# A hybrid decoder block on one Trainium2 core: the gate product in 2x2 blocks with seven block products, its weight sums made by DMA during FF2

## The chip, the core and the metric

The kernel runs on one core of a Trainium2 chip. Its engines are TensorE (PE; its weight loads are listed as PEld), VectorE (DVE), ScalarE (ACT), GpSimd (POOL) and SyncE (SP, which here only issues DMAs). Each works through its own queue of instructions in order; semaphores hold an instruction until what it needs is there, and what stands behind it on that engine waits too. The metric is the device time of one execution in microseconds (us). Times in this document are of the chip.

## What is computed

One decoder layer over 1024 tokens of width 1024 in float32. The last two parts matter here (cut from the reference):

```python
h = h + jnp.concatenate([y_a, y_b, y_c], axis=-1) @ w_out[i]
f = jnp.square(jax.nn.relu(rms_norm(h, norm2_g[i]) @ w_ff1[i]))
h = h + f @ w_ff2[i]
gate = jax.nn.sigmoid(rms_norm(h, norm3_g[i]) @ w_ple_gate[i])
h = h + gate * (p[i] @ w_ple_proj[i])
```

`rms_norm` divides a token's row by the root of its mean square and multiplies by a gain g. `w_ff2` is 4096x1024, `w_ple_gate` 1024x1024.

## The kernel before

Everything is kept transposed: a tile is 128 features by 512 tokens, `h_res[n][h]` is feature block n (0 to 7) of token half h (0 or 1). A float32 product is done as three matmuls on halves of the number: each operand is split into a high part (a copy rounded to `float32r`, by ACT, line 134) and a low part (the rest, by DVE, line 135), and high x high, high x low and low x high are added up in a PSUM bank. There are eight banks. Loads go through SP (`fetch`, `w_pair`), with a pool of buffers for each kind: 4 raw tiles, 22 weight parts, 6 for `sum`, 12 for `tmp`, and 56 slots for h, f and their parts.

*FF1 and FF2 in seven products.* Both work on 2x2 blocks (feature halves by token halves) with seven block products instead of eight, from sums of blocks. FF2's weight sums `w_sums` are made in DRAM by accumulating DMAs of POOL during the attention (`block_sums`); the sums of its other operand are made in FF1 by POOL and stored to `f_dram`. FF2 runs over two chunks c of the inner dimension, in each over seven products p in the order `DOWN`, in each over four output blocks j: 56 steps of 24 matmuls. Products that add to the same bank are mates (`MATE`: 1 and 2, 5 and 3, 7 and 4). Results are added to or taken from `h_res` by DVE (lines 973 to 998), and in the last chunk `finish` squares a finished block on ACT and adds the square to `S3[h]` on POOL.

*The gate.* It is a plain product: for each output block n and token half h 8 x 3 matmuls over all feature blocks k, from parts `h3[k][h]` of h times the gain `g3`, which are split when FF2 is over (line 999). The root of the mean square (`root_of`: four matmuls with a matrix of ones, DVE, a power on POOL, a diagonal on DVE; `spread_root`: a matmul, a copy by ACT to `R3[h]`) is applied after the product, in `gated`: DVE multiplies bank and R3, ACT takes the sigmoid, DVE multiplies by the projection of p (fetched from `pp_dram`) and adds h, and the block is stored, by SP for the last two n and by POOL for the others. The last block goes in two pieces of 256 tokens.

The order of instructions on each engine is fixed at build time by a scheduler that works with its own cost model, from the priorities in which the code is written and from buffers that come free; so code written in one place can stand in another on its engine.

Of the kernel before, what the change touches and what calls it, by code (L numbers as in the profile page):

```python
# [7 lines left out]
F32 = mybir.dt.float32  # L8
# [5 lines left out]
P = 128  # L14
# [3 lines left out]
HT = 512  # L18
# [14 lines left out]
def hybrid_block(ctx: ExitStack, tc: tile.TileContext, a: dict):  # L33
# [92 lines left out]
    g3 = load_const("g3", [P, KT])  # L126
    gq = load_const("gq", [P, 1])
# [790 lines left out]

    h_res = [[None, None] for _ in range(KT)]
    u_sum = [None] * 4  # L920
    h3 = [[None, None] for _ in range(KT)]
    S3 = [late_slot("R", "S3") for _ in range(2)]
    R3 = S3
    DOWN = (1, 5, 2, 3, 6, 7, 4)
    CHUNKS = FT // KC
    steps = [(c, p, j) for c in range(CHUNKS) for p in DOWN for j in range(4)]

    def f_pairs():
        for c in range(CHUNKS):
            for p in DOWN:  # L930
# [33 lines left out]

    seen = [False, False]
    for s, (c, p, j) in enumerate(steps):
# [13 lines left out]
        elif p == 6:  # L980
            subtract(nc.vector, u_sum[j], u_sum[j], bank)
            if last:
                add(nc.vector, h_res[j][1], h_res[j][1], u_sum[j])
                finish(j, 1)
                for h in range(2):
                    t = residual(j + 4, h)
                    subtract(nc.vector, t, t, u_sum[j])
        elif p in (2, 3):
            t = residual(j, p - 2)
            add(nc.vector, t, t, bank)  # L990
            if last and p == 2:
                finish(j, 0)
        else:
            h = 0 if p == 4 else 1
            t = residual(j + 4, h)
            subtract(nc.vector, t, t, bank)
            if last and p != 5:
# [8 lines left out]
    def gated(n, h, g_ps, c):  # L1006
        gt = late_slot("tmp", "gt")[:, c]
        nc.vector.tensor_tensor(out=gt, in0=g_ps, in1=R3[h][:, c], op=ALU.mult)
        nc.scalar.activation(gt, gt, AF.Sigmoid)
        nc.vector.tensor_tensor(out=gt, in0=gt, in1=pps[n, h][:, c], op=ALU.mult)  # L1010
        ot = late_slot("tmp", "ot")[:, c]
        nc.vector.tensor_tensor(out=ot, in0=gt, in1=h_res[n][h][:, c], op=ALU.add)
        queue = nc.sync if n >= KT - 2 else nc.gpsimd
        queue.dma_start(a["out"][n * P:(n + 1) * P, half[h]][:, c], ot)

    pps, undone = {}, []
    for n0 in range(0, KT, 2):
        wus = [plain_units(a["w_ple_gate"][n]) for n in (n0, n0 + 1)]
        for n, h in [(n, h) for h in (1, 0) for n in (n0, n0 + 1)]:
            pps[n, h] = fetch(pp_dram[n][:, half[h]], "sum")  # L1020
            last = n == KT - 1 and h == 0

            for c in (slice(0, 256), slice(256, HT)) if last else (slice(0, HT),):
                g_ps = late_bank("g_ps")[:, c]
                product(g_ps, [(wus[n - n0][k], cols(h3[k][h], c)) for k in range(KT)])
                undone.append((n, h, g_ps, c))
                if n == 0:
                    if h == 0:
                        diag = root_of(S3[0], "30")
                    continue  # L1030
                if n == 1:
                    spread_root(diag, R3[h])
                while undone:
                    gated(*undone.pop(0))
# [62 lines left out]
```

## Time and profile before

| | us |
|---|---|
| three runs | 1264.21, 1258.99, 1256.04 |
| their median | 1258.99 |
| the profiled execution | 1262.6 |
| its span, from first to last instruction | 1260.9 |
| FF2, first to last matmul (span's time) | 860 to 1165 |
| gate stage, to the end of the span | 1165 to 1261 |

The profile is of one execution, with its own time; times in its rows count from the start of its span. A row of a group says line, engine and operation, out<-in by the program's names, the number, and lengths; a row of a wait says who waited for whom, for how long in all and how often. "L135" is line 135 of the kernel above. Idle time of an engine costs only where the others wait for it.

### The profile page before, as it was taken

The numbers are of one execution on the slowest core, as the hardware profiler recorded it, in microseconds if no ns is written. First come the engines' busy times: TensorE is split into PE (matmuls) and PEld (weight loads), VectorE is DVE, ScalarE is ACT, GpSimd is POOL, SyncE is SP. The second block draws the span as 40 slices with busy tenths as digits, with TensorE's granted clock in tenths as the row PEclk, the third lists the DMA queues.
The fourth block names the chain that finished last, engine by engine and source line by source line (L and its number), as shares of the span: only waits on it lengthen the run. The fifth ranks groups of instructions, "written<-read, shape, count | busy, mean of one in ns | idle before, by whom it ended". The sixth has DMA issues, their size and how long they took to land.

```text
span 1260.9 us, 17509 instructions
## 1 busy us (share of the span) xinstructions
PE 1215.0 (96%) x5868; PEld 1034.1 (82%) x5868; DVE 880.7 (70%) x1324; ACT 603.8 (48%) x1167; POOL 364.2 (29%) x365
## 2 busy tenths in 40 slices
PE   9999898899999999879999999999999999999998
PEld 7898798898888878658888888888888888888887
DVE  7746886898979654676887777777755565686443
ACT  7725655666656454553334334344544344555211
POOL 2324434455323212233553453431000000122110
PEclk9999998999999999989999999999999999999999
DMA  9603257788542298689999999958956565653231
GB/s 309 211 18 117 84 158 210 167 210 159 119 114 38 67 292 226 175 221 251 269 244 255 252 244 250 252 193 302 354 179 224 183 223 170 203 166 106 76 111 51
DMA packets 118700, 234.89 MB, mean 186 GB/s; under 512 B 13105, under 2 KB 20529, under 8 KB 118353
## 3 DMA queue, kind: packets, MB, share of 16 engines
q1 hardware_dynamic: 94752, 168.08, 40.4%
q0 software_dynamic: 23856, 65.70, 23.3%
q8 instruction: 46, 0.75, 0.3%
q14 instruction: 46, 0.37, 0.1%
HBM read 176.57 MB, written 78.64 MB: 202 GB/s over the span
## 4 chain that ended last, share of the span: by engine, by line
PE 82%; DVE 8%; DMA 5%; issue 2%; ACT 1%; POOL 1%; SPq 0%; DVEq 0%; POOLq 0%; ACTq 0%
PE d_ps L731 24%; PE f_ps L731 24%; PE qkv_ps L161 3%; PE qkv_ps L162 3%; PE qkv_ps L163 3%; PE g_ps L161 2%; PE g_ps L163 2%; PE g_ps L162 2%; DVE rem L413 2%; PE av L456 2%; DMA S<-sq 2%; PE w_tr L438 1%; PE cv_ps L161 1%; DMA h_dram<-h 1%; PE cv_ps L162 1%
## 5 line engine op out<-in xcount | busy, mean ns | idle before, releaser
L135 DVE TENSOR_TENSOR w_lo<-raw,w_hi 128x512 fp32r<-128x512 f32 x268 | 244.9, 916 | 94.4 <-ACT w_hi L134 92.2
L134 ACT CAST w_hi<-raw 128x512 fp32r<-128x512 f32 x268 | 165.2, 619 | 242.6 <-PE d_ps L731 116.7
L731 PE MATMUL f_ps<-hn_hi,w_hi 128*128 128x512 f32 x448 | 176.5, 394 | 5.3 <-ACT v L884 5.3
L731 PE MATMUL f_ps<-hn_lo,w_hi 128*128 128x512 f32 x448 | 175.7, 392 | 0.0
L731 PE MATMUL f_ps<-hn_hi,w_lo 128*128 128x512 f32 x448 | 175.3, 392 | 0.0
L731 PE MATMUL d_ps<-f_hi,w_lo 128*128 128x512 f32 x448 | 174.3, 389 | 0.0
L731 PE MATMUL d_ps<-f_hi,w_hi 128*128 128x512 f32 x448 | 174.3, 389 | 0.0
L731 PE MATMUL d_ps<-f_lo,w_hi 128*128 128x512 f32 x448 | 174.3, 389 | 0.0
L731 PEld LDWEIGHTS f_ps<-hn_hi,w_hi 128*128 128x128 f32 x448 | 85.1, 190 | 23.4 <-ACT v L884 5.7
L719 POOL TENSOR_TENSOR S<-S,sq 128x512 f32<-128x512 f32 x14 | 22.6, 1614 | 273.5 <-ACT sq L788 273.5
L731 PEld LDWEIGHTS f_ps<-hn_lo,w_hi 128*128 128x128 f32 x448 | 85.1, 190 | 17.9 <-issue 0.2
L731 PEld LDWEIGHTS f_ps<-hn_hi,w_lo 128*128 128x128 f32 x448 | 85.0, 190 | 18.0
L731 PEld LDWEIGHTS d_ps<-f_hi,w_hi 128*128 128x128 f32 x448 | 84.1, 188 | 17.6
L731 PEld LDWEIGHTS d_ps<-f_lo,w_hi 128*128 128x128 f32 x448 | 84.1, 188 | 17.4
L731 PEld LDWEIGHTS d_ps<-f_hi,w_lo 128*128 128x128 f32 x448 | 84.1, 188 | 17.3
L413 DVE TENSOR_TENSOR_SCAN rem<-rem 128x128 f32<-128x128 f32 (+3 forms) x64 | 89.0, 1393 | 11.1 <-ACT rem L409 10.6
L161 PE MATMUL qkv_ps<-whi,xn_hi 128*128 128x384 f32 x256 | 92.0, 359 | 2.6 <-DVE V L138 2.6
L163 PE MATMUL qkv_ps<-whi,xn_lo 128*128 128x384 f32 x256 | 89.8, 351 | 0.0
L162 PE MATMUL qkv_ps<-wlo,xn_hi 128*128 128x384 f32 x256 | 89.8, 351 | 0.0
L135 DVE TENSOR_TENSOR f_lo<-raw,f_hi 128x512 fp32r<-128x512 f32 x112 | 77.6, 723 | 4.6 <-ACT f_hi L134 4.0
L134 ACT CAST f_hi<-raw 128x512 fp32r<-128x512 f32 x112 | 67.0, 620 | 17.9 <-DMA raw<-f_dram 13.4
L416 POOL TENSOR_TENSOR wt<-wt,rem 128x127 f32<-128x127 f32 (+4 forms) x40 | 44.3, 1109 | 107.7 <-DVE rem L413 44.9
(219 smaller groups left out, 2665.7 us busy)
## 6 DMA issues: line engine op xcount, KB each, us to landing
raw<-in_w_ff SPq DMA_DIRECT2D x160, 256.0 KB, 4.1
raw<-f_dram SPq DMA_DIRECT2D x112, 256.0 KB, 4.8
raw<-w_sums SPq DMA_DIRECT2D x64, 256.0 KB, 3.7
f_dram<-f SPq DMA_DIRECT2D x48, 256.0 KB, 4.4
f_dram<-t SPq DMA_DIRECT2D x48, 256.0 KB, 3.9
w_sums<-in_w_ff POOLq DMA_DIRECT2D x8, 1024.0 KB, 11.7
w_sums<-w_sums POOLq DMA_DIRECT2D x8, 1024.0 KB, 12.4
raw<-in_w_ff POOLq DMA_DIRECT2D x32, 256.0 KB, 5.4
```

The source lines that it names most:

```text
L134: nc.scalar.copy(hi, src)
L135: low.tensor_tensor(out=lo, in0=src, in1=hi, op=ALU.subtract)
L161: nc.tensor.matmul(ps, lh, rh, start=first and i == 0, stop=False)
L162: nc.tensor.matmul(ps, lh, rl, start=False, stop=False)
L163: nc.tensor.matmul(ps, ll, rh, start=False, stop=last and i == len(terms) - 1)
L413: nc.vector.tensor_tensor_scan(out=back, data0=back, data1=back, initial=1.0, op0=ALU.mult, op1=ALU.bypass)
L416: done = (nc.vector if on_vector else nc.gpsimd).tensor_tensor(out=wt[:, :W - 1], in0=wt[:, :W - 1], in1=rem[:, 1:W], op=ALU.mult)
L438: nc.tensor.transpose(tr[:, n:n + P], wts[i][:, kb * P:(kb + 1) * P], ident)
L456: nc.tensor.matmul(av[:, first * P:], lhs, part[:, o:o + m], start=kb == 0 and part is hi, stop=kb == 2 * g + 1 and part is lo)
L719: return eng.tensor_tensor(out=out, in0=x, in1=y, op=ALU.add)
L731: nc.tensor.matmul(bank, l, r, start=first and k == 0 and i == 0, stop=k == len(b) - 1 and i == 2, skip_group_check=True)
```

## The change

The gate product is also done with seven block products. With A11 to A22 the blocks of the weight matrix, products 1, 2 and 4 take A11, A12 and A22 as the weight operand, and 5, 6, 7 and 3 take S1 = A21 + A22, S2 = S1 + A11, S3 = A11 + A21 and S4 = S2 + A12; the other operand is blocks of h times `g3` or sums of them, some negated (`minus_g3`), so that every sum is an addition. Three things make the operands:

- *Weight sums.* `gate_sums` makes the four sums in DRAM (`g_sums`) with 32 DMAs of 256 KB through POOL, 16 plain copies and 16 accumulating, two at each of 16 steps of FF2's first chunk, each pair behind a two-column copy on POOL that waits for that step's result.
- *Sums of h.* Four kinds of scaled blocks `hg` (ACT, line 996 of the new code) are added up in place by 16 accumulating DMAs from SBUF to SBUF (`sum_h`), four for each j, each of which needs the one before it for that j to have landed. Products 1, 2 and 3 take single blocks, split as before (`h3_pair`); 6, 5, 7 and 4 take the sums, split by `h3_sum`.
- *FF2's second chunk* runs its products in the order 1, 2, 6, 7, 4, 5, 3, so that token half 0 is done earlier; its root is made within FF2.

The gate's products run in the order 1, 2, 3, 6, 5, 7, 4, each over four output blocks j with 12 matmuls; 7 and 4 do the last block in two pieces.

```diff
+    minus_g3 = const.tile([P, KT], F32, name="minus_g3")
+    nc.vector.tensor_scalar_mul(minus_g3, g3, -1.0)
...
+    G_STEPS = [((0, "A21"), (2, "A11")), ((0, "+A22"), (1, "A11")), ((2, "+A21"), (1, "+S1")),
+               ((3, "A12"), (3, "+S2"))]
+    def gate_sums(i, behind):
+        if not 0 <= i < 16:
+            return
+        paced = nc.gpsimd.tensor_copy(pace, behind[:, :2])
+        with tc.issue_after(paced.ins):
+            for to, what in G_STEPS[i % 4]:
...
+                if what[0] == "+":
+                    nc.gpsimd.dma_start(g_sums[to, j], src, accum_op=ALU.add,
+                                        max_dma_last_dim=2048)
+                else:
+                    nc.gpsimd.dma_start(g_sums[to, j], src)
...
-    DOWN = (1, 5, 2, 3, 6, 7, 4)
+    DOWN = [(1, 5, 2, 3, 6, 7, 4), (1, 2, 6, 7, 4, 5, 3)]
...
+    def scale_h(of, n, h, g):
+        t = scaled[of, n % 4] = slot("hg")
+        nc.scalar.activation(t, h_res[n][h], AF.Copy, scale=g[:, n:n + 1])
+    def h3_pair(p, n, h):
+        h3[p][n % 4] = pair("h3")
+        split(h_res[n][h], *h3[p][n % 4], scale=g3[:, n:n + 1])
+    def sum_h(to, of, j):
+        nc.gpsimd.dma_start(scaled[to, j], scaled[of, j], accum_op=ALU.add)
+    def h3_sum(p, of, j):
+        h3[p][j] = two_parts(scaled[of, j], lambda s: slot(f"h3_{s}", F32R))
...
-    for n, h in [(j + 4 * i, h) for i, h in ((0, 0), (0, 1), (1, 1), (1, 0)) for j in range(4)]:
-        h3[n][h] = pair("h3")
-        split(h_res[n][h], *h3[n][h], scale=g3[:, n:n + 1])
-    diag = root_of(S3[1], "31")
+        if p != 1 and c == 0:
+            gate_sums(s - 12, u_sum[j] if p == 6 else t)
+        if last and p == 5:
+            if j == 1:
+                diag = root_of(S3[0], "30")
+            elif j == 3:
+                spread_root(diag, R3[0])
+        elif last and p == 3:
...
+            for n in range(3) if j == 2 else (3,) if j == 3 else ():
+                scale_h("12", n, 1, minus_g3)
+                sum_h("11", "12", n)
...
+    GATE = (1, 2, 3, 6, 5, 7, 4)
+    MATE = {2: 1, 4: 7}
...
+    for p in GATE:
+        for j in range(4):
+            cs = pieces if p in (7, 4) and j == 3 else whole
...
+            for bank, c in zip(banks, cs):
+                run(bank, w, [cols(b, c) for b in h3[p]], p not in MATE, p not in (1, 7))
+                if p == 1:
+                    v_of[j] = late_slot("tmp", "v")
+                    nc.scalar.copy(v_of[j], bank)
+                elif p == 2:
+                    gated(j, 0, bank, late_slot("tmp", "gt"), c)
+                elif p == 6:
+                    subtract(nc.vector, v_of[j], v_of[j], bank)
+                elif p == 5:
+                    e_of[j] = late_slot("tmp", "e")
+                    add(nc.vector, e_of[j], bank, v_of[j])
+                    t = late_slot("tmp", "gt")
+                    add(nc.vector, t, d_bank.pop((3, j))[0], e_of[j])
+                    gated(j, 1, t, t, c)
+                elif p == 7:
+                    t = e_of[j][:, c]
+                    add(nc.vector, t, bank, t)
+                    gated(j + 4, 1, t, t, c, -1.0)
+                elif p == 4:
+                    t = v_of[j][:, c]
+                    add(nc.vector, t, bank, t)
+                    gated(j + 4, 0, t, t, c, -1.0)
+            if p == 1:
+                if j == 1:
+                    diag = root_of(S3[1], "31")
+                elif j == 3:
+                    spread_root(diag, R3[1])
+                h3_pair(2, j + 4, 0)
+                sum_h("12", "22", j)
+            elif p == 2:
+                h3_pair(3, j + 4, 1)
+                sum_h("22", "11", j)
+            elif p == 3:
+                h3_sum(6, "22", j)
+                sum_h("21", "22", j)
+            elif p == 6:
+                h3_sum(5, "11", j)
...
-        "w_ple_gate": blocks(i["w_ple_gate"][0]),
+        "w_ple_gate": quad_blocks(i["w_ple_gate"][0], 4, 4)[:, 0],
```

How the instructions stand now shows best at three places. On POOL before, around the gate's first stores, there are only the second root r and stores of finished blocks (line numbers of the old code):

```order
L1014 DMA out_T<-ot_11664 128x512
L1014 DMA out_T<-ot_11671 128x512
L169 TENSOR_TENSOR r_11708<-ms_11706,mhalf 128x4
L1014 DMA out_T<-ot_11746 128x512
L1014 DMA out_T<-ot_11753 128x512
```

On POOL in the new order, from the addition of FF2's last square on (line 721; `sq_11616` is of the last step) to the last of the sums (line 1003; `hg_11532` is the last j of the sum that product 6 takes; line numbers of the new code, as in the next fences):

```order
L721 TENSOR_TENSOR S_1911_8639<-S_1911_8639,sq_11616 128x512
L1003 DMA hg_11588<-hg_11530 128x512
L1003 DMA hg_11524<-hg_11619 128x512
L1003 DMA hg_11576<-hg_11528 128x512
L1003 DMA hg_11530<-hg_11522 128x512
L171 TENSOR_TENSOR r_11682<-ms_11680,mhalf 128x4
L1003 DMA hg_11619<-hg_11532 128x512
L1003 DMA hg_11578<-hg_11530 128x512
L1003 DMA hg_11532<-hg_11524 128x512
L1003 DMA hg_11580<-hg_11532 128x512
```

The root for token half 1 stands between sums, each of which waits for the landing of another: `hg_11530` is read by the first sum and written by the fourth, `hg_11619` is written by the one after r, and `hg_11532` needs that one and the second.

On DVE before, at the second half's first evictions, rows of the gate stand beside weight parts, one bank read for every three rows:

```order
L1008 TENSOR_TENSOR gt_11742<-g_ps_11676,S_1910_8634 128x512
L1010 TENSOR_TENSOR gt_11742<-gt_11742,raw_11674 128x512
L1012 TENSOR_TENSOR ot_11746<-gt_11742,h_9156 128x512
L1008 TENSOR_TENSOR gt_11749<-g_ps_11714,S_1910_8634 128x512
L1010 TENSOR_TENSOR gt_11749<-gt_11749,raw_11712 128x512
L1012 TENSOR_TENSOR ot_11753<-gt_11749,h_9207 128x512
```

On DVE in the new order, from the diagonal of the root (which waits for r above) to the first block that is gated (line 1074; `h_lo<-hg` is the low part of a sum of h):

```order
L808 TENSOR_TENSOR diag_11684<-ident,r_11682 128x512
L140 SCALAR_TENSOR_TENSOR h_lo_11804<-h_9005,c_g_115,h_hi_11803 128x512
L140 SCALAR_TENSOR_TENSOR h_lo_11835<-h_9057,c_g_115,h_hi_11834 128x512
L137 TENSOR_TENSOR w_lo_11970<-raw_11967,w_hi_11969 128x512
L140 SCALAR_TENSOR_TENSOR h_lo_11866<-h_9109,c_g_115,h_hi_11865 128x512
L137 TENSOR_TENSOR h_lo_11890<-hg_11526,h_hi_11889 128x512
L137 TENSOR_TENSOR w_lo_11994<-raw_11991,w_hi_11993 128x512
L137 TENSOR_TENSOR h_lo_11914<-hg_11528,h_hi_11913 128x512
L137 TENSOR_TENSOR h_lo_11938<-hg_11530,h_hi_11937 128x512
L137 TENSOR_TENSOR h_lo_11962<-hg_11532,h_hi_11961 128x512
L1074 TENSOR_TENSOR gt_11766<-g_ps_11628,S_1910_8638 128x512
```

The low part of `hg_11532`, the sum that lands last, now stands ahead of the first gated block, and the diagonal ahead of three of the four parts for product 3.

The end of DVE's queue in the new order, from the read of the last bank (the second 256-wide piece of product 4's last block) on:

```order
L721 TENSOR_TENSOR v_11736<-g_ps_12292,v_11736 128x256
L1074 TENSOR_TENSOR v_11736<-v_11736,S_1910_8638 128x256
L1076 TENSOR_TENSOR v_11710<-v_11710,raw_12399 128x512
L1074 TENSOR_TENSOR v_11736<-v_11736,S_1910_8638 128x256
L1076 TENSOR_TENSOR v_11736<-v_11736,raw_12419 128x256
L721 TENSOR_TENSOR v_11710<-v_11710,h_10112 128x512
L721 TENSOR_TENSOR v_11736<-v_11736,h_10166 128x256
L1076 TENSOR_TENSOR v_11736<-v_11736,raw_12419 128x256
L721 TENSOR_TENSOR v_11736<-v_11736,h_10166 128x256
```

Behind that read stand eight more rows, of both pieces and of the block before; before the change three stood behind the last read.

More of the change, by code (lines that the diff above doesn't have):

```diff
@@ L963, in finish @@
         seen[h] = True
+    h3 = {p: [None] * 4 for p in range(1, 8)}
+    scaled = {}
+    def scale_h(of, n, h, g):
[8 more added lines that the diff above has]
+        h3[p][j] = two_parts(scaled[of, j], lambda s: slot(f"h3_{s}", F32R))
     seen = [False, False]
@@ L990, in hybrid_block @@
             add(nc.vector, t, t, bank)
[L991 to L992 removed]
+            if last:
+                finish(j, p - 2)
         else:
@@ L996, in hybrid_block @@
             subtract(nc.vector, t, t, bank)
-            if last and p != 5:
+            if last and p != 7:
                 finish(j + 4, h)
-    for n, h in [(j + 4 * i, h) for i, h in ((0, 0), (0, 1), (1, 1), (1, 0)) for j in range(4)]:
-        h3[n][h] = pair("h3")
-        split(h_res[n][h], *h3[n][h], scale=g3[:, n:n + 1])
-    diag = root_of(S3[1], "31")
[L1006 to L1034, printed above, removed]
+        if p != 1 and c == 0:
+            gate_sums(s - 12, u_sum[j] if p == 6 else t)
```

57 lines of the change are left out of this document (53 added, 4 removed).

## The prediction, made before the changed kernel had run

> **What bounds the kernel now.** I read the page's first parts, then a table of stages, then the product's own rows, and last the waits of the engines that feed it. First the page: the span, the busy time of each engine, and the shares of the chain that ended last.
>
> ```profile
> span 1260.9 us, 17509 instructions
> PE 1215.0 (96%) x5868; PEld 1034.1 (82%) x5868; DVE 880.7 (70%) x1324; ACT 603.8 (48%) x1167; POOL 364.2 (29%) x365
> PE 82%; DVE 8%; DMA 5%; issue 2%; ACT 1%; POOL 1%; SPq 0%; DVEq 0%; POOLq 0%; ACTq 0%
> ```
>
> TensorE carries the end. The stage table (from:to, length, then busy us of PE, PEld, DVE, ACT and POOL, the granted clock, the share of the DMA engines, GB/s) shows the same for a stretch of FF1, two of FF2 and the gate stage:
>
> ```profile
> 600.00:700.00 100.00, 100.00 (x443) 82.84 (x442) 81.26 (x84) 35.98 (x62) 49.83 (x46) 1.00 0.95 255
> 925.00:1012.00 87.00, 87.00 (x385) 72.07 (x384) 49.43 (x78) 36.78 (x62) 0.00 (x0) 1.00 0.60 203
> 1012.00:1165.00 153.00, 153.00 (x679) 126.73 (x677) 103.67 (x153) 75.17 (x127) 21.10 (x13) 1.00 0.53 173
> 1165.00:1261.00 96.00, 91.06 (x429) 75.68 (x427) 41.19 (x63) 16.31 (x27) 10.21 (x15) 0.99 0.23 80
> ```
>
> PE is never idle in FF2 and has 91 of the gate stage's 96 us; DVE is busy in 41 of them, the DMA engines in 23%. So fewer matmuls shorten the gate stage as long as DVE, POOL and the sums keep up. The rows of the two products, and two of the 256-wide matmuls at the end:
>
> ```profile
> L731 PE MATMUL d_ps<-f_hi,w_hi x448: 389/389/390, 860.2 to 1164.2; 128*128 128x512 f32 x150
> L731 PE MATMUL d_ps<-f_hi,w_lo x448: 389/389/390, 860.7 to 1164.6; 128*128 128x512 f32 x150
> L163 PE MATMUL g_ps<-h_hi,w_lo x136: 279/389/398, 1166.2 to 1255.8; 128*128 128x512 f32 x120, 128*128 128x256 f32 x16
> 1250.38 0.28 PE L163 MATMUL g_ps<-h_hi,w_lo 128*128 128x256 f32 x1
> 1250.50 0.28 PE L161 MATMUL g_ps<-h_hi,w_hi 128*128 128x256 f32 x1
> ```
>
> FF2's 3 x 448 = 1344 matmuls last from 860.2 to 1164.6 + 0.4 = 1165.0, so a 512-wide one costs 304.8 / 1344 = 0.227 us; a 256-wide one starts 0.12 after the one before. The gate stage is 360 of the first and 48 of the second kind.
>
> **The matmuls that go.** Seven products of four blocks with 12 matmuls are 336 full ones, of which 24 are cut into 48 halves as before. 312 stay whole: 48 x 0.227 = 10.9 us less on PE. The norm's matmuls stay, a pair of groups like these moving into FF2:
>
> ```profile
> 1165.00 0.79 PE ms_ps L798 x8
> 1176.84 0.86 PE R_ps L813 x2
> ```
>
> PE's gate stage goes from 360 x 0.227 + 48 x 0.12 + 2 x 1.65 = 90.8 us (measured 1165.0 to 1256.1, 91.1) to 79.9; of these 1.65 now lie in FF2, so it ends 78.3 us after FF2's last matmul.
>
> **What DVE gets to do.** Its speed, in rows of start, length, line:
>
> ```profile
> 1165.04 0.69 DVE L716 TENSOR_TENSOR h<-h,d_ps 128x512 f32<-128x512 f32 x1 [0.48 <-PE d_ps L731]
> 1165.64 0.68 DVE L135 TENSOR_TENSOR w_lo<-raw,w_hi 128x512 fp32r<-128x512 f32 x1
> 1166.25 0.16 DVE L801 TENSOR_SCALAR ms<-ms_ps 128x4 f32<-128x4 f32 x1
> 1240.86 0.69 DVE L1010 TENSOR_TENSOR gt<-gt,raw 128x512 f32<-128x512 f32 x1 [0.70 <-ACT gt L1009]
> 1241.58 0.69 DVE L1012 TENSOR_TENSOR ot<-gt,h 128x512 f32<-128x512 f32 x1
> L138 DVE SCALAR_TENSOR_TENSOR h_lo<-h,c_g,h_hi x16: 739/744/1784, 1124.4 to 1167.1; 128x512 fp32r<-128x512 f32 x16
> ```
>
> An operation is 0.69 long, but the next starts 0.60 after it if it doesn't need its result (1165.04 to 1165.64), and 0.72 if it does (1240.86 to 1241.58). After FF2's last step the new order has 121 on DVE: 96 full ones, the diagonal among them (96 x 0.60 = 57.6), 8 of the scaled kind (8 x 0.74 = 5.9), 16 halves (16 x 0.43 = 6.9, lengths in the next fence) and one of 0.16, some 12 of them 0.12 longer for their operand: 72.0 us, against 78.3 on PE. DVE has 6 us to spare, no more; had each cost 0.72, DVE would be the bound. ACT's 80 at 0.63 (sq below) are 50 us, so it has room.
>
> **The tail.** Now, behind the last matmul (1256.1):
>
> ```profile
> 1256.10 0.42 DVE L1008 TENSOR_TENSOR gt<-g_ps,S 128x256 f32<-128x256 f32 x1 [1.08 <-PE g_ps L163]
> 1257.00 0.43 DVE L1010 TENSOR_TENSOR gt<-gt,raw 128x256 f32<-128x256 f32 x1 [0.48 <-ACT gt L1009]
> 1257.46 0.42 DVE L1012 TENSOR_TENSOR ot<-gt,h 128x256 f32<-128x256 f32 x1
> ```
>
> It is 1.8 us to the end of DVE, and 3.0 more to the span's end for the store, which stays. In the new order eight DVE rows stand behind the last read of a bank, six halves and two whole ones, since the two pieces and the block before them are interleaved: 0.43 + 6 x 0.43 + 2 x 0.60 = 4.2, and some 0.5 of backlog from product 5 (five rows for a block, 3.1 us, against 2.7 of PE). So +2.9 us.
>
> **The sums of h by DMA.** Sixteen accumulating DMAs of 256 KB, SBUF to SBUF, go through POOL's queue, with the squares' additions and the root r between them, so one late sum holds all behind it. The like in this trace: S<-sq with its landing, raw<-raw, and for contrast a plain store of POOL and a load of SP; then what stands between the sums.
>
> ```profile
> L790 POOL DMA_DIRECT2D S<-sq x14: 843/857/892, 457.7 to 548.1; - x14
> DMA to landing us min/median/max: 3.4/5.2/8.0
> raw<-raw POOLq DMA_DIRECT2D x32, 256.0 KB, 5.2
> out_T<-ot POOLq DMA_DIRECT2D x12, 256.0 KB, 2.4
> raw<-in_w_ple_gate SPq DMA_DIRECT2D x16, 256.0 KB, 2.6
> L719 POOL TENSOR_TENSOR S<-S,sq x14: 1283/1398/3350, 1068.6 to 1167.5; 128x512 f32<-128x512 f32 x14
> L169 POOL TENSOR_TENSOR r<-ms,mhalf 128x4 f32<-128x4 f32 x2 | 2.1, 1035 | 3.8 <-DVE ms L801 3.7
> L788 ACT ACTIVATE sq<-h x28: 614/632/635, 456.7 to 1165.8; 128x512 f32<-128x512 f32 x28
> ```
>
> I followed POOL's rows one by one with a landing time L, an issue of 0.87, an addition of 1.3 and the root of 1.04. The first sum leaves 11.7 us before FF2's end, as soon as its square and the one before are added. Six landings then stand in a row (each reads or overwrites the one before, or is behind such a one in the queue), with 7.2 us of issues, additions and the root between them and 0.7 for the cast: DVE can take the last block of product 6, the row that waits longest, at 6L - 3.8 after FF2's end, and has 102 rows from there (86 x 0.60 + 12 x 0.12 + 16 x 0.43 = 60). DVE's end by this chain is 6L + 56.2; PE's chain gives 78.3 + 0.5 (PE's wait for the root's matmul, behind r in POOL's queue; 0 to 1) + 4.7 = 83.5. They meet at L = 4.5. Ends of L: 3.4 and 5.2 as a median. In the two stages of those rows the DMA engines are near full (0.95 in 600 to 700), in the gate stage 0.23 before and, with the sums, more weights and as many stores, perhaps half; I take L = 4.0, nearer the low end, and PE's chain holds.
>
> [...]
>
> **The weight sums in FF2.** 32 DMAs of 256 KB, DRAM to DRAM, half of them accumulating, and 16 tiny copies on POOL that pace them, in steps 12 to 27 of the first chunk, 925 to 1012, where POOL is idle (0.00 in the table). Their like are the 1 MB sums of FF2's own weights; beside them what SP's queue took in that window, and what ACT waits for in FF2:
>
> ```profile
> w_sums<-in_w_ff POOLq DMA_DIRECT2D x8, 1024.0 KB, 11.7
> w_sums<-in_w_ff POOLq DMA_DIRECT2D x16, 7.0
> q1 hardware_dynamic: 13438, 24.47, 63.3%
> ACT w_hi L134 <- PE d_ps L731: 116.7, 63, 2.1
> ```
>
> By a quarter of these landings they take up to 16 x 1.8 + 16 x 2.9 = 75 us of the window's 87; by bytes (SP moves 24.5 MB in 63% of 87 us, 0.45 MB/us; these are 8 MB) at least 18. What covers them is that ACT waits 116.7 us in FF2 for PE to free weight buffers: operands stand ready ahead of need. FF1 runs at a share of 0.95 with PE at 100%. I take 0, between 0 and the price of the third case.
>
> **The rest.** The second chunk's new order has the same matmuls, DMAs and additions; the 16 SP loads of each product only move with it, and the gate's first weights stay behind the last of them: 0. The 16 scaled copies lie on ACT, idle half of FF2. The new DVE operation at the start is 0.16 long in an engine that waits for loads there: 0. Twelve more gate weight loads on SP (28 against 16) at 2.6 us each run ahead of PE.
>
> Sum: -10.9 + 2.9 + 0.5 = -7.5. The profiled execution took 1262.6 (its span and 1.7 around it), so 1255.1; it lies 3.6 above the median of 1258.99, and against that the time is 1251.5.
>
> **Rivals.** *Slow sums, DVE the bound.* At L = 5.2 DVE ends 87.4 + 1.65 after FF2's old end instead of 92.9 (1257.9 - 1165.0): -3.8, 1255. At 8.0, the longest landing, +13, 1272. For it: two groups with a median of 5.2. Against: emptier engines. It decides from 4.5 on.
>
> *FF2 starved, the other side.* If the sums keep POOL's ring busy for 75 us and SP's gets half of each engine then, SP's 55 us (63% of 87) find 37 + 12 = 49: 6 short, and at a third 25 + 12 = 37: 18 short, because the accumulating packets are the slower ones. What the buffers held ahead don't cover, PE loses: -7.5 + 6 to + 18, 1257 to 1269, slower than before from a loss of 7.5 on. Against it: the 116.7 us of waiting for buffers. [...]
>
> *The whole saving.* If DVE keeps pace to the end the tail is 2.3 (one operation more): -10.9 + 0.5 = -10.4, 1248.6. The interleaved last rows speak against it.
>
> **The numbers.** The sum with its own bounds (1248 to 1255) has 0.60, slow sums 0.20, FF2 starved 0.13, the whole saving 0.07. The range 1246 to 1261 leaves out the far ends of the second and third. A measurement of this kernel tells about 1% from no change (12.6 us). Nearly all cases lie within it: 0.90; faster by more needs the whole saving and a low median, 0.05; slower takes the far ends, 0.05.
>
> **What would show it.** PE's gate rows end 78 to 80 us after FF2's last; FF2 lasts 306 to 307 us, with the norm's matmuls in it; sums land in 3.4 to 4.5; DVE is busy nearly without a gap from 25 us into the gate stage and ends 4 to 5 us behind PE. I am wrong if PE waits for the low parts of h or w in the gate stage, if DVE's end is 8 us or more behind PE, or if FF2 is longer than 308 us.

## The result and the profile after

The changed kernel takes 1251.85 us (median of 8 runs, 1249.81 to 1253.73), the kernel before 1261.21 in its 8 (1256.04 to 1264.21): a ratio of 0.9934 with a 95% interval of 0.9917 to 0.9952, so 6 to 10.5 us less, 8.3 in the middle. The page of the changed kernel, its span and its engines:

```profile
span 1250.1 us, 17694 instructions
PE 1202.6 (96%) x5820; PEld 1024.0 (82%) x5820; DVE 907.5 (73%) x1374; ACT 626.7 (50%) x1212; POOL 407.7 (33%) x432
```

TensorE still carries the span, with 48 matmuls less for the gate. The rows of the two products (number, lengths, first and last start), and the one wait of TensorE in the gate stage (who for whom, us in all, times, longest):

```profile
L733 PE MATMUL d_ps<-f_hi,w_hi x448: 389/389/791, 856.2 to 1162.0; 128*128 128x512 f32 x150
L733 PE MATMUL d_ps<-f_hi,w_lo x448: 388/389/397, 856.6 to 1162.5; 128*128 128x512 f32 x150
L733 PE MATMUL g_ps<-h_hi,w_lo x120: 279/389/796, 1163.1 to 1242.6; 128*128 128x512 f32 x104, 128*128 128x256 f32 x16
```

```profile
PE R_ps L815 <- DVE diag L808: 1.4, 1, 1.4
```

FF2 lasts from 856.2 to 1162.9 (the last start and 0.4), 306.7; the gate product ends at 1242.6 + 0.28 = 1242.9, 80.0 after it. VectorE's last rows:

```profile
1242.45 0.42 DVE L721 TENSOR_TENSOR v<-g_ps,v 128x256 f32<-128x256 f32 x1
1242.79 0.68 DVE L721 TENSOR_TENSOR v<-v,h 128x512 f32<-128x512 f32 x1
1243.38 0.42 DVE L721 TENSOR_TENSOR v<-g_ps,v 128x256 f32<-128x256 f32 x1
...
1246.72 0.42 DVE L721 TENSOR_TENSOR v<-v,h 128x256 f32<-128x256 f32 x1
```

It ends at 1247.1, 4.3 behind TensorE, and the span 2.9 later with the store. By stages, in the two profiled executions:

| us | before | after | difference |
|---|---|---|---|
| FF2 | 304.8 | 306.7 | +1.9 |
| FF2's last matmul to the gate's last | 91.1 | 80.0 | -11.1 |
| from there to VectorE's end (the tail) | 1.8 | 4.3 | +2.5 |
| from there to the end of the span | 3.0 | 2.9 | -0.1 |
| FF2's start to the end of the span | 400.7 | 393.9 | -6.8 |

The spans differ by 10.8; the other 4.0 lie ahead of FF2, where the two kernels have the same order but for one operation of 0.16 us. Over the fourteen executions profiled here FF2 starts anywhere between 853.6 and 862.1, so those 4 us are taken as scatter, and the change is read from FF2's start on. Next the sums of h with their landing, and three rows of VectorE's timeline (start, length, operation, idle time before it and who ended it): the first waits for one of these sums, the other two for TensorE.

```profile
L1003 POOL DMA_DIRECT2D hg<-hg x16: 859/880/1561, 1149.3 to 1187.0; - x16
DMA to landing us min/median/max: 3.3/4.8/6.3
```

```profile
1187.36 0.69 DVE L137 TENSOR_TENSOR h_lo<-hg,h_hi 128x512 fp32r<-128x512 f32 x1 [4.50 <-ACT h_hi L136]
...
1237.32 0.69 DVE L721 TENSOR_TENSOR v<-g_ps,v 128x512 f32<-128x512 f32 x1 [0.15 <-PE g_ps L733]
...
1240.04 0.69 DVE L721 TENSOR_TENSOR v<-g_ps,v 128x512 f32<-128x512 f32 x1 [0.49 <-PE g_ps L733]
```

They land in 4.8 (median), not in 4.0; the low part of the last block for product 6 comes 1187.36 - 1162.9 = 24.5 after FF2. From there VectorE is busy nearly without a gap until it waits 0.15 and 0.49 for TensorE. The chain of the end, in order of time (start, length, what), shows what stands before TensorE's 1.4 us:

```profile
1170.08 4.86 DMA hg<-hg
1174.93 0.28 issue
1175.22 0.86 POOL hg L1003
1176.08 1.07 POOL r L171
1177.15 0.02 issue
1177.17 0.70 DVE diag L808
1177.88 0.04 issue
1177.92 1.13 PE R_ps L815 x2
1179.05 60.98 PE g_ps L733 x280
```

A sum on POOL waits for another sum's landing, the root r stands behind it in the queue, and diag and TensorE wait for r. The window of the weight sums and the gate stage (columns as in the prediction's table of stages):

```profile
925.00:1012.00 87.00, 87.00 (x386) 72.06 (x385) 48.78 (x77) 35.77 (x60) 27.42 (x47) 1.00 0.94 283
...
1163.00:1250.00 87.00, 78.43 (x370) 65.12 (x368) 71.21 (x121) 37.91 (x67) 20.72 (x29) 0.98 0.58 160
```

The weight sums bring the DMA engines to a share of 0.94, and TensorE has no gap. The 0.58 of the gate stage is a mean over a busy beginning and a quieter end; while the sums of h run, around TensorE's wait, the share is higher:

```profile
1170.00:1174.00 4.00, 4.00 (x19) 3.31 (x18) 1.83 (x4) 3.91 (x7) 2.65 (x3) 1.00 0.91 192
1174.00:1177.00 3.00, 2.48 (x11) 1.70 (x10) 0.00 (x0) 1.66 (x4) 1.78 (x3) 1.00 1.12 202
1177.00:1179.00 2.00, 1.08 (x3) 0.60 (x4) 1.83 (x3) 0.24 (x1) 1.03 (x2) 1.00 0.86 153
1179.00:1182.00 3.00, 3.00 (x15) 2.46 (x14) 3.00 (x6) 0.38 (x1) 1.73 (x2) 1.00 0.90 128
```

(The share is worked out from the times of packets and comes out above 1 in places.)

### The profile page after: what moved, and what is told of

Its sections match the earlier page's. It is cut to its first block, busy times and chain, and to the rows that moved or that the text cites. A ratio compares the mean times of both kernels' runs of the same rounds, so it can differ in the third digit from the quotient of the medians.

```text
span 1250.1 us, 17694 instructions
## 1 busy us (share of the span) xinstructions
PE 1202.6 (96%) x5820; PEld 1024.0 (82%) x5820; DVE 907.5 (73%) x1374; ACT 626.7 (50%) x1212; POOL 407.7 (33%) x432
## 5 line engine op out<-in xcount | busy, mean ns | idle before, releaser
L137 DVE TENSOR_TENSOR w_lo<-raw,w_hi 128x512 fp32r<-128x512 f32 x280 | 249.7, 894 | 92.9 <-ACT w_hi L136 92.3
L136 ACT CAST w_hi<-raw 128x512 fp32r<-128x512 f32 x280 | 171.8, 618 | 215.8 <-PE d_ps L733 118.4
L733 PEld LDWEIGHTS d_ps<-f_lo,w_hi 128*128 128x128 f32 x448 | 84.1, 188 | 17.8 <-issue 0.2
L733 PEld LDWEIGHTS d_ps<-f_hi,w_hi 128*128 128x128 f32 x448 | 84.1, 188 | 17.6 <-ACT hg L996 0.2
L733 PEld LDWEIGHTS d_ps<-f_hi,w_lo 128*128 128x128 f32 x448 | 84.1, 188 | 17.4
L171 POOL TENSOR_TENSOR rs<-ss,mhalf 128x4 f32<-128x4 f32 x32 | 44.4, 1389 | 75.9 <-DVE ss L341 72.4
```

The source lines that it names most:

```text
L136: nc.scalar.copy(hi, src)
L137: low.tensor_tensor(out=lo, in0=src, in1=hi, op=ALU.subtract)
L171: nc.gpsimd.tensor_tensor(out=out, in0=in_, in1=mhalf[:, :n], op=ALU.pow)
L733: nc.tensor.matmul(bank, l, r, start=first and k == 0 and i == 0, stop=k == len(b) - 1 and i == 2, skip_group_check=True)
```

## The experiments

The changed kernel and twelve others, each against the kernel before, with the stages of one profiled execution each (us; "VectorE's end" counts from FF2's last matmul, "rest" from there to the end of the span):

| kernel | ratio, 95% interval | FF2 | gate on TensorE | tail | VectorE's end | rest |
|---|---|---|---|---|---|---|
| changed kernel | 0.9934, 0.9917 to 0.9952 | 306.7 | 80.0 | 4.3 | 84.2 | 2.9 |
| no_h_sums | 0.9947, 0.9929 to 0.9966 | 306.7 | 78.4 | 4.2 | 82.6 | 5.3 |
| late_root | 1.0010, 0.9998 to 1.0022 | 306.7 | 88.3 | 4.3 | 92.5 | 2.9 |
| no_w_sums | 0.9928, 0.9903 to 0.9952 | 306.7 | 79.9 | 4.2 | 84.1 | 4.0 |
| w_sums_twice | 0.9956, 0.9937 to 0.9974 | 307.6 | 81.2 | 4.3 | 85.4 | 3.0 |
| root_first | 0.9928, 0.9909 to 0.9947 | 306.7 | 78.4 | 4.3 | 82.7 | 2.9 |
| extra_landing | 0.9943, 0.9921 to 0.9964 | 306.6 | 79.4 | 4.3 | 83.7 | 2.9 |
| tail_whole | 0.9946, 0.9925 to 0.9967 | 306.7 | 79.2 | 4.1 | 83.3 | 3.3 |
| reorder_only | 1.0029, 1.0014 to 1.0044 | 306.7 | 95.4 | 1.9 | 97.2 | 3.0 |
| sums_on_dve | 0.9963, 0.9943 to 0.9982 | 306.7 | 81.8 | 4.3 | 86.1 | 6.2 |
| block_last | 0.9957, 0.9938 to 0.9975 | 306.7 | 80.7 | 2.4 | 83.1 | 6.8 |
| late_sums | 0.9974, 0.9957 to 0.9990 | 306.7 | 84.4 | 4.3 | 88.7 | 2.9 |
| best | 0.9944, 0.9921 to 0.9967 | 306.6 | 79.0 | 2.4 | 81.4 | 6.8 |

The stages scatter too. Five kernels besides the changed one have its order on POOL and TensorE up to the root of token half 1. TensorE's wait at R_ps is 1.44 in the changed kernel and 1.29, 0.53, 0.73 and 0.31 in no_w_sums, extra_landing, tail_whole and late_sums; in w_sums_twice it is not there, but TensorE stops 0.98 at ms_ps, the matmuls before the root. The order is the same and the waits are not, so a difference of a microsecond between two gate stages is not yet an effect of the edit.

**no_h_sums.** `sum_h` does nothing.

```diff
-        nc.gpsimd.dma_start(scaled[to, j], scaled[of, j], accum_op=ALU.add)
+        pass
```

> Leaves out the sixteen accumulating DMAs that add up the blocks of h, so products 6, 5, 7 and 4 work on single scaled blocks. In the changed kernel 84.2 us pass from FF2's last matmul to the end of VectorE. Theory A (TensorE's chain carries; the sums cost only the 1.4 us that TensorE waits at R_ps for the root that stands behind them on POOL): TensorE's gate part 80.0 -> 78.6, VectorE still ends about 4.3 behind it, 84.2 -> 82.8, the time 1.4 shorter. Theory B (the sums bind through VectorE, which waits 4.5 us for one of them): VectorE ends under 3 us behind TensorE and the 84.2 go below 80.5, the time about 4 shorter.

Theory A holds: 78.4, no wait of TensorE, and a tail of 4.2. VectorE now waits for TensorE (its waits in the gate stage):

```profile
DVE v L718 <- PE g_ps L733: 5.9, 4, 1.6
...
DVE e L721 <- PE g_ps L733: 1.4, 1, 1.4
```

So without the sums VectorE has 7.3 us to spare in products 6 and 5, and the tail is the same with that and without: it isn't work left over from the products before. Only the total doesn't follow (0.9947): the rest is 5.3 instead of 2.9 (last section).

**late_root.** The root of token half 1 later in the code.

```diff
-                if j == 1:
-                    diag = root_of(S3[1], "31")
-                elif j == 3:
-                    spread_root(diag, R3[1])
 ...
                 sum_h("22", "11", j)
+                if j == 3:
+                    diag = root_of(S3[1], "31")
 ...
                 sum_h("21", "22", j)
+                if j == 3:
+                    spread_root(diag, R3[1])
```

> The root of token half 1 and its spreading come later in the code, behind the sums of h (same work, same result). Theory A (TensorE's chain carries, and its 1.4 us at R_ps are the root's place in POOL's queue): no wait at R_ps, TensorE's gate part 80.0 -> 78.6, and since the sums also come 1.1 earlier without the root between them, VectorE's end 84.2 -> 82.8. Theory B (VectorE is already the bound, by the sums): TensorE ends 1.4 earlier but VectorE only 1.1 at most, so its distance behind TensorE grows. Rival C (the wait at R_ps is not POOL's queue): R_ps still waits 1 us or more.

All three theories missed what the edit did: ms, which r needs, came late on VectorE, r stood on POOL behind two stores that wait for VectorE, and TensorE met R_ps before it:

```profile
1197.35 0.15 DVE L803 TENSOR_SCALAR ms<-ms_ps 128x4 f32<-128x4 f32 x1
1197.59 5.63 POOL L171 TENSOR_TENSOR r<-ms,mhalf 128x4 f32<-128x4 f32 x1 [1.08 <-DVE ms L803]
1204.00 2.07 PE L815 MATMUL R_ps<-diag,ones 128*128 128x512 f32 x2 [7.15 <-DVE diag L808]
```

The two stores were out by 1196.5; what r waited for last is ms. It then lasted 5.63, where the six of the changed kernel and the six of the kernel before take 1.0 to 1.9; why is not known, and without it the wait of 7.15 would be some 4 shorter. So the run shows that a late root stops TensorE, but not what this place in the queue alone costs. The gate is 88.3 - 78.4 = 9.9 longer for a wait of 7.15, and the whole gain is gone. The other 2.7 are the clock, at half until 1209 (last section).

**no_w_sums and w_sums_twice.** The weight sums left out, and made twice.

```diff
-        if not 0 <= i < 16:
-            return
+        return
         paced = nc.gpsimd.tensor_copy(pace, behind[:, :2])
 ...
-    ... else g_sums[int(of[1]) - 1, j]
+    ... else w_block("w_ple_gate", "A11", j)
```

```diff
-                if what[0] == "+":
-                    nc.gpsimd.dma_start(g_sums[to, j], src, accum_op=ALU.add, max_dma_last_dim=2048)
+                for sums in (g_sums, g_twin):
+                    if what[0] == "+":
+                        nc.gpsimd.dma_start(sums[to, j], src, accum_op=ALU.add, max_dma_last_dim=2048)
```

> Leaves out the weight sums (the 32 DMAs and 16 paced copies in FF2); the products that need them read another block of the weights. Theory A (the weight sums cost FF2 nothing, though the DMA engines are at a share of 0.94 there): FF2 stays 306.7 within 0.3 and the time within 1 us. Theory B (they starve FF2 a little): FF2 shorter by 0.5 us or more.

> Makes every weight sum twice (a second copy that nobody reads): 64 DMAs instead of 32 in the same steps. By the changed kernel's shares in the window (54% for SP's queue, 39% for POOL's) they want 54 + 79 = 133% of 87 us. Theory A (SP's loads get their turn and only the sums fall behind; weight parts stand ready ahead of need): FF2 stays 306.7 to 307.7. Theory B (loads and sums share the engines alike): SP's queue loses, TensorE waits in FF2, which grows by 5 us or more.

Left out: FF2 is 306.7 as with them (theory A), at a share of 0.61 instead of 0.94 in the window. Twice, in the same window of that run (922 to 1009):

```profile
922.00:1009.00 87.00, 87.00 (x385) 72.06 (x384) 39.99 (x63) 27.62 (x49) 39.16 (x68) 1.00 1.03 307
```

The engines are full, TensorE still has no gap there, and the sums fall behind: the last one is issued at 1037 instead of 1016. The loads of SP's queue fall behind too: ACT's wait for TensorE to free weight buffers, the sign that operands stand ready ahead of need, shrinks from 118.4 over FF2 in the changed kernel to 48.0, and it waits 44.3 for loads of `w_ff` instead. So the stock of parts covers the sums, and doubled they have used up more than half of it; FF2 loses 0.9 later (307.6, within theory A), 0.7 of it behind VectorE. Already the single sums make SP's loads slower: from 925 to 1012 those of `w_ff` land in 5.0 (median) in the changed kernel and in 2.9 in the kernel before, those of `f_dram` in 6.8 and 5.0. How the DMA engines divide their time between the two queues was not shown. The gate stage of this run, 81.2, holds the stop of 0.98 at ms_ps and a stretch at half clock behind it (last section).

**root_first.** One sum issued behind r instead of before it.

```diff
+                if j == 2:
+                    with tc.issue_after(root_ops["31"].ins):
+                        sum_h("22", "11", j)
+                else:
+                    sum_h("22", "11", j)
-                sum_h("22", "11", j)
```

> One sum of h (the one that waits on POOL for another's landing just ahead of the root r of token half 1) is issued after r instead of before it; all else is unchanged. In the changed kernel r starts at 12.9 us after FF2's last matmul, TensorE waits 1.4 at R_ps. Theory A (TensorE's chain carries, the wait is r's place in POOL's queue): r starts 2.5 to 3 us earlier, no wait at R_ps, TensorE's gate part 80.0 -> 78.4 to 78.7, VectorE's end 84.2 -> 82.6 to 82.9, the time 1.4 shorter. Theory B (VectorE is bound by the sums at their landing of 4.8): TensorE gains 1.4, VectorE not more than the 1.1 by which the sums behind r move up, and its waits at the end are gone. Rival C (something else holds R_ps): no change.

Theory A holds: no wait, 78.4, 82.7, so 1.5 us shorter by the stages of one execution each; after the scatter above, the gain can be less in others. The runs (0.9928 against 0.9934) can't tell so little.

**extra_landing and late_sums.** The last sum for product 6 done twice, and four times.

```diff
                 sum_h("22", "11", j)
+                if j == 3:
+                    sum_h("22", "11", j)
```

> Makes one more sum of h, a repeat of the last one for product 6 (so that block of h is wrong), which waits for the first to land: one landing more in the chain that VectorE waits for, 5.9 us by the changed kernel's POOL rows, behind r and so without effect on R_ps. VectorE waits 4.5 us for this sum there and again 0.15 and 0.49 for TensorE just before the end. Theory A (those 0.64 are all that VectorE has to spare, the forecast's 6 us used up by the landing of 4.8 instead of 4.0): VectorE's gap 4.5 -> 10.4, its end 84.2 -> 89.5 after FF2's last matmul, the time 5 longer. Theory B (it has the forecast's 6 us to spare even now): no change over 1 us.

> Makes the last sum of h for product 6 four times instead of once (that block of h is wrong), each behind the landing of the one before: by the kernel with one repeat (3.5 us) some 11 us later. The order on VectorE moves 11 rows (6.6 us) ahead of the row that waits, so 11 - 6.6 = 4.4 are left of it. Theory A (VectorE has only the 0.64 us to spare that it waits for TensorE near the end): its end 84.2 -> 87.5 to 88.5 after FF2's last matmul, TensorE's last products waiting for it less than 1, the tail growing from 4.3. Theory B (VectorE has the forecast's 6 us to spare): 84.2 within 1.

One repeat landed in 3.5, and the scheduler, which sees it, moved three of VectorE's rows (1.8) ahead of the one that waits: the test was too weak, 83.7. With four the row comes 35.6 after FF2 instead of 24.5; less the 6.6 of rows moved ahead, VectorE is 4.5 late. The end is 88.7, within a little of A's number, but not by A's way: the tail is 4.3 as ever. TensorE waits instead, for a bank that VectorE reads too late:

```profile
1214.80 0.76 PE L733 MATMUL g_ps<-h_hi,w_hi 128*128 128x512 f32 x1 [3.65 <-DVE v L718]
```

4.5 late and 3.65 waited: by this, an estimate from two executions, VectorE had about 0.9 to spare at a landing of 4.8. That is near the 0.64 that it waits for TensorE in the changed kernel, and neither the forecast's break-even of 4.5 nor 6 us.

**tail_whole.** The last blocks of products 7 and 4 in one piece.

```diff
-            cs = pieces if p in (7, 4) and j == 3 else whole
+            cs = whole
```

> Products 7 and 4 do their last block whole instead of in two pieces (same result). Tail from TensorE's last matmul to VectorE's end, 4.3 now. Theory A (the forecast's: the tail is the number of rows behind the last read of a bank, eight now; whole, the block before is done in TensorE's 2.7 us and four rows and a sigmoid are left): 0.05 + 0.72 + 0.72 + 0.65 + 0.72 + 0.69 = 3.5 to 3.8; TensorE itself 24 x 0.227 - 48 x 0.12 = 0.3 shorter; the time 0.5 to 1.1 shorter. Theory B (the pieces pay, as for a plain product): the tail 5 or more, the time 0.5 longer or more.

Neither: 4.1. From the last read on there are six rows, two of them still of the block before, since the scheduler interleaves them; I had counted four. The pieces hardly matter.

**reorder_only.** The kernel before with only FF2's new order, the root of half 0 in FF2, and the gate's blocks in the order half 0, half 1 (the lines shown are of the first two).

```diff
-    DOWN = (1, 5, 2, 3, 6, 7, 4)
+    DOWN = [(1, 5, 2, 3, 6, 7, 4), (1, 2, 6, 7, 4, 5, 3)]
 ...
+        if last and p == 5:
+            if j == 1:
+                diag = root_of(S3[0], "30")
+            elif j == 3:
+                spread_root(diag, R3[0])
```

> The kernel before with FF2's second chunk in the new order and the root of token half 0 inside FF2, and the plain gate product with half 0 first: neither sums of h nor of weights, no seven products. Theory A (the order costs nothing): FF2 304.8 -> 306.5 with the norm's matmuls in it, TensorE's gate part 91.1 -> 89.4, tail 1.8, so FF2's start to the end of the span 400.7 within 0.7 and the time within 1.5 of the kernel before. Theory B (the reorder brings part of the gain or takes some): more than 2 us either way, by TensorE waiting less or more at the gate's start for h or the root.

FF2 as expected, but the gate is 6.0 longer than expected: the squares of half 1 now end FF2, and TensorE stops for them at once (rows of windows; TensorE's clock is the last but two):

```profile
1166.60 1.81 PE L800 MATMUL ms_ps<-ones,S 128*128 128x2 f32 x8 [2.85 <-POOL S L721]
```

```profile
1163.80:1166.60 2.80, 0.00 (x1) 0.00 (x1) 2.09 (x3) 1.67 (x3) 1.26 (x1) 1.00 0.48 136
1166.60:1169.00 2.40, 2.40 (x10) 2.30 (x11) 0.66 (x2) 0.00 (x0) 0.31 (x1) 0.52 0.17 63
1169.00:1172.00 3.00, 3.00 (x9) 2.32 (x8) 0.69 (x1) 0.00 (x0) 0.71 (x1) 0.50 0.00 0
1172.00:1175.00 3.00, 3.00 (x12) 2.37 (x11) 0.00 (x0) 0.00 (x0) 0.00 (x0) 0.75 0.00 0
1175.00:1178.00 3.00, 3.00 (x15) 2.49 (x14) 0.83 (x2) 0.63 (x1) 0.00 (x0) 1.00 0.00 0
```

That is 2.85 of waiting, and the stretch at half clock behind it makes up the other 3. In the changed kernel the same root hides behind the 48 matmuls of product 1. So the order by itself gains nothing, and what covers it is the new gate.

**sums_on_dve, block_last, best.** Three kernels, each built on the one ahead of it. In sums_on_dve VectorE does the first four sums of h. In block_last, besides, the last block of product 2, which needs one VectorE row less, is done at the very end, in two pieces, and stored by SP. In best, besides, no sum that waits for a landing stands on POOL ahead of the last square or the root: the last sum for product 6 goes behind r, as in root_first, and the four for product 4 behind that one. The main lines of the three edits:

```diff
-                sum_h("11", "12", n)
+                add(nc.vector, scaled["11", n], scaled["11", n], scaled["12", n])
```

```diff
-    for p in GATE:
-        for j in range(4):
+    STEPS = [(p, j) for p in GATE for j in range(4) if (p, j) != (2, 3)] + [(2, 3)]
+    for p, j in STEPS:
```

```diff
+                with tc.issue_after(last_sum.ins):
+                    sum_h("21", "22", j)
-                sum_h("21", "22", j)
```

> The first four of the sixteen sums of h (block 11 plus 12, three of them still inside FF2) are additions of VectorE instead of DMAs; twelve DMAs stay. Theory A (TensorE's chain carries; the sums matter through POOL's queue ahead of r and through VectorE's gap): the chain of landings is one shorter, so r is out by the time that TensorE wants it (R_ps waits 0 to 0.5), TensorE's gate part 78.4 to 79, VectorE's gap before the last block of product 6 falls from 4.5 to under 1 although it has 4 x 0.6 more to do, and its end comes 82.6 to 83.2 after FF2's last matmul instead of 84.2. Theory B (what VectorE is given decides): 2.4 us more work, end 84.2 or later.

> As the kernel with four sums on VectorE; besides, the last block of product 2 is done at the very end, in two pieces, instead of behind the other three of its product (same result). It needs three VectorE rows for a piece, where product 4 needs four, and the block ahead of it is whole. Theory A (the tail is the VectorE rows behind the last read of a bank): four of 0.34 to 0.6 behind the last read, with the sigmoid: tail 2.0 to 2.6 instead of 4.3, TensorE as in the kernel with four sums on VectorE (it waits for no bank, though one is held longer), VectorE's end 80.5 to 81.5 after FF2's last matmul, the time 3 shorter than the changed kernel's. Theory B (the bank held to the end makes TensorE wait for VectorE to free another in products 6 and 5): TensorE 2 us or more later, nothing gained.

> The last block of product 2 at the very end and the first four sums of h on VectorE, as before, and on POOL no sum that waits for a landing stands ahead of the last square or the root any more: the four sums for product 4 go last, the last one for product 6 behind r (same result). If the three findings add up (root's wait 1.4, tail 4.3 -> 2.4, and squares late on POOL cost the two kernels before this one 1.5 to 1.6 and in one of them a halved clock): TensorE waits at most 0.5 in the gate stage, its part 78.4 to 79.2, tail 2.2 to 2.6, VectorE's end 80.6 to 81.8 after FF2's last matmul (84.2 in the changed kernel), the time 2.5 to 3.5 shorter than the changed kernel's. If VectorE's 2.4 us more work or the held bank bind instead: TensorE waits 1 us or more for a bank, and the end is 82.5 or later.

sums_on_dve: VectorE's gap went, and its work fitted, but the last square now stood on POOL behind a sum that waits, so TensorE stopped 1.6 at ms_ps instead of R_ps, and the clock halved: 81.8. Neither theory had that. block_last: the tail is 2.4, as A has it, with TensorE at 80.7 (1.5 at ms_ps, 0.5 for the held bank). best has both, 79.0 + 2.4 = 81.4, within what was expected: 2.8 less than the changed kernel at VectorE's end. Its time is not less, 0.9944, and here the expectation missed: the rest is 6.8 instead of 2.9. Nothing here beats the changed kernel in the runs by more than they can tell.

## Why the prediction was right, step by step

It said 1251.5; the median is 1251.85, and the sum of -7.5 stands against -6.8 from FF2's start on and -8.3 by the ratio. That the times agree within 0.4 is luck: the forecast started from 1258.99, the median of three runs, and the median of the eight is 1261.21, so the medians are 9.4 apart, and a base 2.2 too low made up for a change 1.9 too small. What holds is the size of the change and how it is made up. The steps, by their names there:

*The matmuls that go.* Right: 78.3 was worked out for a TensorE that waits for nothing, and where it doesn't (no_h_sums, root_first) it is 78.4. FF2 with the norm's matmuls is 306.7.

*What DVE gets to do.* Right: 121 rows in the gate stage, and without the sums 7.3 us of waiting for TensorE in products 6 and 5, where 6 to spare were forecast.

*The tail.* 4.3 for 4.7. The last read of a bank starts 0.5 behind TensorE (1243.38), as much as the forecast had put down as backlog from product 5. But it isn't backlog: the tail is 4.1 to 4.3 in every kernel that ends with product 4, whether VectorE has 7 us to spare or none, and what stands ahead of that read are rows of product 4 itself (1242.45 and 1242.79). The nine rows from there on took 3.8 instead of 4.2, because a row of 256 starts 0.34 after another of its kind and not 0.43, its length. *The whole saving* needed a tail of 2.3; it took another order to come near it, with three rows behind the last read (block_last, best: 2.4).

*The sums of h by DMA.* Here a size was off, and the reason for it was wrong. The landing was taken as 4.0, because the DMA engines would be emptier than in the stages of the like; the median was 4.8, outside the forecast's own sign (3.4 to 4.5). The engines weren't emptier: from 1149 to 1188, while the sums run, their share is 0.83, and 0.58 of it is POOL's queue, which is the sums themselves. And the like had been read at the wrong place: S<-sq ran from 457 to 548, where the share is 0.80, not at the 0.95 of 600 to 700. The formula held: 6 x 4.8 - 3.8 = 25.0 for the row that measured 24.5.

TensorE's wait for the root was put at 0.5 (0 to 1). In the changed kernel's profile it is 1.4, and against the kernel without the sums and the one with r ahead of one sum it costs 1.6. In the other kernels with the same order up to the root it was 0.3 to 1.3, or 1.0 at ms_ps, so 0.5 was a fair middle and the bound too narrow: r stands behind a sum that itself waited 1.7 to 2.6 for a landing in these six kernels.

The case *slow sums, DVE the bound* didn't come, though 4.8 is past the forecast's 4.5, where the two chains were to meet. They nearly do: VectorE had some 0.6 to 0.9 left, and when it has none TensorE stops for a bank (late_sums); VectorE's end isn't what moves first.

*The weight sums in FF2.* Right, and shown by leaving them out; *FF2 starved* has no room, since even twice as many cost 0.9. The half and the third that it left to SP's queue were suppositions: SP's queue kept 54.3% of the DMA engines' time beside 39.3% for POOL's (925 to 1012 in the changed kernel, 59.5% before without the sums). The packets of POOL's queue are the slower ones, 0.17 us each against 0.10 of SP's from 1140 to 1200, while the sums of h run (an estimate from each queue's packets and share). The estimate by bytes rested on a wrong window: the row with 24.47 MB and 63.3% is of 900 to 1012. For the 87 us from 925 on it is 17.59 MB at 59.5%, which makes at least 25 us for the sums instead of 18, and 52 us for SP's loads instead of 55. The forecast of 0 didn't hang on it.

*The rest.* Right for the changed kernel; but "the order costs nothing" holds only with the new gate behind it (reorder_only). And the store "which stays" had less cover than I knew: see below.

So -10.9 by the matmuls, +1.6 for the root, +2.5 for the tail is -6.8 in the two profiled executions: the expected loss in the tail came 0.4 smaller, the one on POOL's queue 1.1 larger, and the two misses partly cancel.

## What to carry to other kernels

When a chain of small dependent DMAs shares a queue with something that TensorE waits for, put the short work first: on POOL, which works in order, a landing of 4.86 ahead of the root became a stop of TensorE of 1.44, and with the sum behind the root (root_first) there was none. A faster algorithm on TensorE can show its price in the tail (here 4.3 for 1.8) and in the spare time of the engine behind it (here some 0.9 us are left to VectorE, the estimate of late_sums); count the rows behind the last read of a bank, and look for banks that are read late, not for the other engine's end. Read a change of 0.6% from the stage that it touches, and then check that the program really ends where that stage does. And where a forecast says that a resource will be emptier, count what the change itself puts on it (here 0.58 of a share of 0.83).

## What the runs showed of the hardware

*A short stop can halve TensorE's clock.* The granted clock by windows in sums_on_dve, where TensorE stops for 1.64 at ms_ps, in block_last, where it stops at the same place for 1.50, and in w_sums_twice, where it stops there for 0.98:

```profile
1174.00:1176.00 2.00, 0.36 (x3) 0.16 (x2) 2.00 (x2) 1.94 (x4) 1.92 (x3) 1.00 1.06 255
1176.00:1178.00 2.00, 2.00 (x13) 1.78 (x14) 2.00 (x5) 1.63 (x3) 1.63 (x2) 0.98 0.90 159
1178.00:1181.00 3.00, 3.00 (x8) 2.32 (x7) 0.42 (x1) 0.10 (x1) 1.20 (x2) 0.50 1.07 216
```

```profile
1171.00:1173.00 2.00, 0.77 (x7) 0.77 (x7) 2.00 (x2) 2.00 (x5) 2.00 (x3) 1.00 1.08 277
1173.00:1175.00 2.00, 2.00 (x11) 1.70 (x11) 1.80 (x4) 1.15 (x2) 0.90 (x2) 1.00 0.95 143
1175.00:1178.00 3.00, 3.00 (x14) 2.47 (x14) 0.00 (x0) 2.01 (x4) 1.92 (x2) 1.00 0.99 210
```

```profile
1164.00:1167.00 3.00, 2.63 (x12) 1.86 (x10) 2.67 (x3) 2.34 (x5) 1.60 (x2) 1.00 1.05 221
1167.00:1170.00 3.00, 2.39 (x13) 2.11 (x14) 3.00 (x5) 3.00 (x6) 1.61 (x3) 0.86 0.87 178
1170.00:1173.00 3.00, 3.00 (x10) 2.33 (x9) 0.78 (x2) 0.37 (x2) 1.61 (x2) 0.57 0.85 158
1173.00:1176.00 3.00, 3.00 (x15) 2.45 (x14) 0.00 (x0) 2.48 (x5) 1.78 (x3) 1.00 1.13 204
```

The first loses another 1.8 (81.8 - 78.4 - 1.64). The second loses nothing to the clock, which stays at 1.00. The third, with the shortest stop of all, loses 1.7 by its two rows below 1.00 (3 x 0.14 + 3 x 0.43), and 78.4 + 0.98 + 1.7 = 81.1 is nearly its whole gate stage of 81.2. Stops of 2.85, 3.65 and 7.15 (reorder_only, late_sums, late_root) all go with 0.50; the changed kernel's 1.44 at the root is followed by 1.00. So between 1 and 1.6 the length of the stop doesn't decide, and what does stays open: a wait like the changed kernel's can come at twice its price (1.64 and another 1.8 in sums_on_dve).

*GpSimd's closing instruction can outlast the stores.* The rest after VectorE's end is 2.9 to 3.0 in the changed kernel and six of the others, and 3.3 in tail_whole, whose last store is a whole block; it is 4.0, 5.3, 6.2, 6.8 and 6.8 in five. In best the last store has landed 5.0 before the span ends, and the records of POOL's sequencer show its closing instruction, a drain, still running. In all five the span ends 0.8 after that drain. From the end of POOL's last DMA issue to the end of that drain, beside the number of DMAs that POOL has issued in the whole program:

```
DMAs   us to the drain's end
154    4.95 (before), 4.98 (reorder_only)
173    5.99 (no_w_sums)
189    7.30 (no_h_sums)
200    8.20 (block_last), 8.20 (best)
201    8.28 (sums_on_dve)
204    3.66 (tail_whole)
205    3.75 (changed kernel), 3.75 (root_first), 3.74 (late_root)
206    3.83 (extra_landing)
208    2.33 (late_sums)
237    3.43 (w_sums_twice)
```

The same number of DMAs gives the same drain within 0.03 and other numbers anything from 2.3 to 8.3: in these executions it goes with that number but not in step with it (8.28 at 201, 3.66 at 204), and what sets it stays open. In the kernel before, POOL's last store is so early that the drain is covered. In the changed kernel the drain ends 0.9 before the last store has landed; in best it ends 4.2 after, which takes back best's 2.8 us and 1.1 more. Late stores by SP instead of POOL would be the next thing to try; that wasn't tried.
